# Low parts of 24 up-projection weight tiles by adding transfers, and weight sums on VectorE

## The chip, the cores and the metric

The kernel runs on one core of one Trainium2 chip. A core has five engines that work at the same time, each through its own list of instructions in order: TensorE (PE, matrix products; PEld is its loading of the stationary operand), VectorE (DVE), ScalarE (ACT), GpSimd (POOL) and SyncE (SP), which here only issues transfers. Transfers (DMA) move data between the device memory and the on-chip memory; a plain one is issued by SP here, one that adds to what already lies at its destination by GpSimd. Engines wait for each other through semaphores. The metric is the device time of one execution in microseconds (us); the median over several runs counts.

## The reference

One layer of a hybrid decoder: 512 tokens, 1024 channels, float32. A convolution branch and a gated linear attention branch run side by side and are merged, and a channel mixer follows. The change is in the mixer:

```python
u2 = _rmsnorm(h, norm2_g[l])
z = _causal_dwconv(u2 @ w_ffn_up[l], ffn_dw_w[l], ffn_dw_b[l])
h = h + (jax.nn.silu(z[..., :FFN_DIM]) * z[..., FFN_DIM:]) @ w_ffn_down[l]
```

FFN_DIM is 2816, so `w_ffn_up` is 1024 x 5632, that is 44 column tiles of 128. Tiles 0 to 21 give the half that goes through silu (called a here), tiles 22 to 43 the half that multiplies it (b); tile f and tile 22 + f belong together. The convolution in between has three taps over time.

## The kernel before

**Products in three parts.** TensorE multiplies in a rounded float32 format (fp32r). To keep precision, each operand is cut in a high part (the value rounded to fp32r) and a low part (what rounding left over). A product x y is then high x high + high x low + low x high, three matrix products in the same accumulator (`mm3`, lines 448 to 450). For an up tile of 1024 x 128 against 512 tokens, `col_tile` (line 452) makes 8 x 3 = 24 products of 128x512, in the order low weight, then twice high weight, for each of the eight blocks of 128 input channels.

**Weights.** Every weight tile is 128 x 1024 floats (512 KB). `load` (line 242) issues its transfer from SP into one of four `raw` buffers. `split_weight` (line 343) makes the two parts, `whi` and `wlo`, in four buffers each: ScalarE copies `raw` into `whi` with rounding (line 385, or 355 for tiles that belong to a pair or to the down projection), and VectorE subtracts `whi` from `raw` into `wlo` (line 390, or 356). For the tiles in the set `ADDED` (some tiles of the input projections) the low part is made otherwise: ScalarE writes the negated rounded value into `wlo` (line 387), and GpSimd issues a second transfer of the same weights that adds to it (line 388). So these tiles are loaded twice, and VectorE has no work for them.

```python
            if (name, spec) in ADDED:
                pace[0] = nc.scalar.mul(lo, raw, -1.0)
                nc.gpsimd.dma_start(lo, a[name][spec], accum_op=ALU.add)
            else:
                pace[0] = nc.vector.tensor_tensor(lo, raw, hi.bitcast(F32), ALU.subtract)
```

**Order.** `order` lists all weights in the order of use. `weight` (line 408) hands out the next one and calls `prefetch` so that two more (`LOOK`) behind it are split, in program order, ahead of the products that follow. `refill` then loads into free raw buffers.

**The up projection.** It is done in three groups (`GROUPS`, line 34) of four, three and four pairs of tile numbers; after each group comes the part of the down projection that uses it (`seven`, line 1370). `up_plan` (line 156) writes the order within a group by hand. The first members of the pairs, and a few more tiles, are plain: a and b each by `col_tile`. The second member q of most pairs is done together with its b tile by `two_tiles` (line 1171), which multiplies the two tiles by two halves of the tokens with seven products instead of eight, on sums and differences of the operands. Its four steps are called x1, x3, x2, x4; their products are 128x256. A unit interleaves these four steps with the pieces of two plain tiles. A unit that closes a group looks like this:

```python
                a1, a2, a3 = (("tile", a, ks) for ks in halves(3, 6))
                seq = [x1, a1, x3, a2, x2, a3, x4, ("second", q), ("tile", b, whole)]
```

so the b tile comes as a whole, directly after x4. In the order of weights it is x1, a, x3, x2, b, x4: b is split when x2 is handed out. In groups one and two these closing tiles are a = 8, b = 30 and a = 12, b = 34; in group three there is no closing unit, and plain tiles 19 and 41 end it. Groups two and three open with a plain tile a (9 and 13), followed by x1 of a pair.

**Weight sums of a pair.** The steps x3 and x4 need sums of quarters of the two raw weight tiles. `two_sums` (line 324) makes four sums of 128x512 per pair on GpSimd (line 327): three behind the split of x1, one behind the split of x3. Eight pairs of up tiles are done this way, and six pairs of merge weights earlier in the kernel.

**Behind the products.** ScalarE and VectorE read the accumulators: bias and three taps of the convolution (lines 1497 and 1500), silu (1508), product of the halves (1514), and then the high and low parts of the activations and of their sums for the down projection (`fsplit`, lines 1519 and 1520: the tiles yh and yl, ah and al, sh and sl, made from w, f and v; line 1530 makes the difference in w). ScalarE also copies partial results of a pair from the accumulators (line 1178), and VectorE combines them (1181). Accumulators are banks of PSUM: five of `mm` and three of `ax`.

Who comes first on an engine where program order does not say it is decided by a scheduling layer at build time; `tc.keep_in_program_order` and `tc.issue_after` tie single instructions to a place.

Of the kernel before, what the change touches and what calls it, by code (L numbers as in the profile page):

```python
# [10 lines left out]
F32 = mybir.dt.float32  # L11
# [6 lines left out]
P = 128  # L18
D = 1024
# [19 lines left out]
BEHIND = [_HALVES[:3], _HALVES[3:6], _HALVES[6:9], _HALVES[9:]]  # L39
BEHIND += [[("w_conv", m, half) for m in pair for half in range(2)] for pair in O_PAIRS[:2]]  # L40
MERGE_REST = [("w_conv", m) for pair in O_PAIRS[2:] for m in pair]
LOOK = 2

ADDED = {("w_glu", 2 * k) for k in range(2, KT)} | {("w_r", m) for m in range(KT)}
ADDED |= {("w_v", KT // 2 + j) for j in (0, 1)}
RATE = 5.0
WARM = (6, 3, 2)
MID = 4
# [27 lines left out]
def trunk_layer(ctx: ExitStack, tc: tile.TileContext, a: dict, out: bass.AP):  # L76
# [24 lines left out]
    def nm(s):  # L101
        return f"{s}_{next(names)}"
# [50 lines left out]
        nc.gpsimd.memset(att, 0.0)  # L153


    def up_plan(gi):


        pairs = GROUPS[gi]
        whole = range(KT)  # L160

        def halves(*cuts):
            return [range(a, b) for a, b in zip((0, *cuts), (*cuts, KT))]

        def unit(q, f, kind):

            a, b = f, FT + f
            x1, x3, x2, x4 = (("part", q, part) for part in ("x1", "x3", "x2", "x4"))
            a1, a2 = (("tile", a, ks) for ks in halves(4))
            if kind == "opens":  # L170
                b1, b2, b3 = (("tile", b, ks) for ks in halves(4, 6))
                seq = [a1, x1, a2, x3, b1, x2, b2, x4, ("second", q), b3]
            elif kind == "closes":
# [3 lines that stand above are left out]
                a1, a2 = (("tile", a, ks) for ks in halves(5))  # L177
                b1, b2 = (("tile", b, ks) for ks in halves(4))
                seq = [x1, a1, x3, a2, x2, b1, x4, ("second", q), b2]
            return seq + [("first", f)]  # L180

        firsts = [p for p, _ in pairs[1:]]
        if gi + 1 < len(GROUPS):
            firsts.append(GROUPS[gi + 1][0][0])
        plan = []
        n = 0
        if gi == 0:
            (p, q), (f, _) = pairs[1:3]
            for i, role in ((p, "first"), (q, "second"), (f, "first")):
                plan += [("tile", i, whole), ("tile", FT + i, whole), (role, i)]  # L190
            n = 2
        while n < len(firsts):
            last = n + 1 == len(firsts) and gi + 1 < len(GROUPS)
            kind = "closes" if last else "opens" if n == 0 else ""
            plan += unit(pairs[n][1], firsts[n], kind)
            n += 1
        if n < len(pairs):
            q = pairs[n][1]
            plan += [("tile", q, whole), ("tile", FT + q, whole), ("second", q)]
        return plan  # L200
# [123 lines left out]
    def two_sums(name, p, q, part):  # L324

        def add(out, x, y):
            work = nc.gpsimd.tensor_tensor(out, x, y, ALU.add)  # L327
            if name == "w_up":
                tc.keep_in_program_order(work)

        left, right = slice(0, T), slice(T, D)
        if part == "x1":
            one, two = pair_raws[name, p]
            three = raw_tile()
            pair_raws[name, p].append(three)
            add(three[:, left], one[:, left], two[:, left])
            add(three[:, right], three[:, left], two[:, right])
            add(two[:, left], two[:, left], two[:, right])
        if part == "x3":
            one, _, three = pair_raws[name, p]  # L340
            add(three[:, left], three[:, right], one[:, right])

    def split_weight(halves=False, between=None):

        if len(ready) < len(order):
            while len(raws) <= len(ready):
                load()
            raw = raws[len(ready)]
            name, spec = order[len(ready)]
            if name in SEVEN or name == "two":  # L350
                raw = operand(raw, *spec) if name in SEVEN else two_operand(*spec)
                n = raw.shape[-1]
                hi = wp.tile([P, D], F32R, tag="whi", name=nm("whi"), bufs=4)[:, :n]
                lo = wp.tile([P, D], F32R, tag="wlo", name=nm("wlo"), bufs=4)[:, :n]
                nc.scalar.copy(hi, raw)  # L355
                two_low[:] = [nc.vector.tensor_tensor(lo, raw, hi.bitcast(F32), ALU.subtract)]  # L356
                with ExitStack() as order_of:
                    for ins in behind:
                        order_of.enter_context(tc.issue_after(ins.ins))
                    sum_on(name, *spec) if name in SEVEN else two_sums(*spec)  # L360
                ready.append((hi, lo))
                refill()
                return
            hi = wp.tile([P, D], F32R, tag="whi", name=nm("whi"), bufs=4)
            if order[len(ready)][0] == "w_low":
                nc.scalar.copy(hi, raw)
                if order[len(ready)][1] == 0:
                    part_lo = lambda t: t.rearrange("p (k c) -> p k c", c=P)[:, :, :RANK]
                    nc.vector.tensor_tensor(part_lo(hi), part_lo(raw), part_lo(hi.bitcast(F32)), ALU.subtract)
                ready.append((hi, None))  # L370
                refill()
                return
            lo = wp.tile([P, D], F32R, tag="wlo", name=nm("wlo"), bufs=4)
            if halves:
                ready.append((hi, lo))

                def high(c):
                    nc.scalar.copy(hi[:, c], raw[:, c])

                def low(c):  # L380
                    nc.vector.tensor_tensor(lo[:, c], raw[:, c], hi[:, c].bitcast(F32), ALU.subtract)

                cols = [slice(j * T, (j + 1) * T) for j in range(2)]
                return [[lambda c=c, part=part: part(c) for c in cols] for part in (high, low)]
            nc.scalar.copy(hi, raw)  # L385
            if (name, spec) in ADDED:
                pace[0] = nc.scalar.mul(lo, raw, -1.0)  # L387
# [3 lines that stand above are left out]
            ready.append((hi, lo))  # L391
            refill()
# [6 lines left out]
    def third_ahead():  # L399

        n = used[0] + LOOK
        if n == len(ready) < len(order) and order[n][0] == "two" and order[n][1][-1] == "x3":
            split_weight()
            return two_low[0]

    two_low = []

# [44 lines left out]
    def col_tile(w, acts, acc=None, lo=0, hi=T, at={}, ks=range(KT)):  # L452

        if acc is None:
            acc = mm_bank()
        for k in ks:
            s = slice(k * P, (k + 1) * P)
            ah, al = acts[k]
            mm3(acc[:, lo:hi], (w[0][:, s], w[1][:, s]), (ah[:, lo:hi], al[:, lo:hi]), k == 0, k == KT - 1)
            if k in at:  # L460
                at[k]()
        return acc

    def row_half(name, j0, n, acts, nk, done, tok_inner, middle=None):

# [702 lines left out]

    combined = []

    def two_tiles(name, p, q, acts7, side_bank, at_once=False):

        x, y, z = mm_bank(), side_bank(), side_bank()
        c1, c2 = tmp(), tmp()
        t1, t2 = slice(0, H), slice(H, T)

# [13 lines left out]
        combine(c1[:, t1], c1[:, t1], z[:, :H], ALU.add)  # L1190
        yield
        w = weight("two", (name, p, q, "x3"))
        step(x, "n2", w, 1, False)
        put(c2[:, t1], x)
        step(y, "s1", w, 0, True)
# [429 lines left out]
    for gi, pairs in enumerate(GROUPS):  # L1625
# [26 lines left out]
        for what, i, *rest in up_plan(gi):  # L1652
            if what == "tile":
                if 0 in rest[0]:
                    banks[i] = (weight("w_up", i), mm_bank())
                wt, acc = banks[i]
                col_tile(wt, acts2, acc, ks=rest[0])
                if KT - 1 in rest[0] and i < FT:
                    values[i] = value(i, acc)
            if what == "part":  # L1660
                if rest[0] == "x1":
                    units[i] = two_tiles("w_up", i, FT + i, lambda: up_acts, ax_bank)
                done = next(units[i])
                if done:
                    values[i] = value(i, done[0])
                    banks[FT + i] = (None, done[1])
                    third = [taps_at[0], third_ahead()]
            if what == "first":
                w = first_gated(i, values.pop(i), banks.pop(FT + i)[1])
                if any(i in pair for pair in pairs):  # L1670
# [105 lines left out]
```

## Time and profile before

| | |
|---|---|
| median of 3 runs | 825.09 us (824.46 to 825.40) |
| profiled execution, its own time | 826.27 us |
| its span, first to last instruction | 824.5 us |
| TensorE busy | 816.3 us, 99% of the span |
| VectorE busy | 719.2 us, 87% |
| ScalarE busy | 449.8 us, 55% |
| GpSimd busy | 148.9 us, 18% |
| granted TensorE clock, mean of the span | 0.999 of full speed |
| data moved by DMA | 106.27 MB, 129 GB/s |

The page of the profile gives busy times of each engine, then the chain of work that ended last, followed back from the last instruction to what released each step, and then groups of instructions: line, engine, operation, output <- inputs with shapes, count, and behind the bar the busy time of the group in us, the mean time of one in ns, and the idle time of the engine just before them with who ended it. Rows of a timeline give start in us, duration in us, engine, line, operation and tiles; in brackets the idle time before and who ended it. Rows of windows give, for a stretch of time, its length and the busy time and count of each engine, the granted clock, the mean busy share of the DMA engines and GB/s. A matrix product's time in a row (0.39 us for 128x512) is longer than the step from one to the next (0.23 us), as they overlap.

### The profile page before, as it was taken

How to read it: one execution, taken by the hardware profiler on the slowest of the kernel's cores; microseconds unless marked ns; L12 is line 12 of the kernel's file. 1: busy time of each engine (PE TensorE's matmuls, PEld its weight loads, DVE VectorE, ACT ScalarE, POOL GpSimd, SP SyncE). 2: the span in 40 equal slices, each digit the busy share in tenths (PEclk: the TensorE clock that was granted, in tenths of full speed). 3: DMA queues.
4: the chain of work that ended last, by engine and by line, in shares of the span. 5: the costliest groups of instructions: out<-in, count | busy, mean ns of one | idle time of the engine just before them, and what ended most of it. 6: DMA issues, size and time to landing. Idle time of an engine off the chain costs nothing.

```text
span 824.5 us, 11562 instructions
## 1 busy us (share of the span) xinstructions
PE 816.3 (99%) x4323; PEld 705.8 (86%) x4323; DVE 719.2 (87%) x1165; ACT 449.8 (55%) x666; POOL 148.9 (18%) x133
## 2 busy tenths in 40 slices
PE   9999999999999999999999999999999999999996
PEld 8888888888888889999988898898889988899885
DVE  5689999998989699886788889989975999789896
ACT  6744446655654456684454546556435663456654
POOL 2000010001010213443001100230123301622012
PEclk9999999999999999999999999999999999999999
DMA  8355673553443103323647633055642457334662
GB/s 317 94 118 150 153 184 103 128 153 103 89 116 103 51 27 114 116 78 106 211 112 215 177 101 103 27 167 160 143 132 89 140 142 164 105 103 148 184 128 103
DMA packets 30616, 106.27 MB, mean 129 GB/s; under 512 B 3464, under 2 KB 3600, under 8 KB 30560
## 3 DMA queue, kind: packets, MB, share of 16 engines
q1 hardware_dynamic: 24784, 85.34, 30.3%
q0 software_dynamic: 5760, 20.19, 14.4%
q8 instruction: 34, 0.56, 0.3%
q14 instruction: 22, 0.18, 0.1%
q10 hardware_dynamic: 16, 0.00, 0.0%
HBM read 103.42 MB, written 2.10 MB: 128 GB/s over the span
## 4 chain that ended last, share of the span: by engine, by line
PE 98%; DMA 0%; ACT 0%; DVE 0%; POOL 0%; POOLq 0%; issue 0%; ACTq 0%
PE mm L448 28%; PE mm L449 28%; PE mm L450 28%; PE mm L662 3%; PE ax L450 2%; PE ax L449 2%; PE ax L448 2%; PE ax L1067 1%; PE ax L576 1%; PE ax L1048 1%; PE ax L1069 1%; PE ax L1035 1%; DMA x<-in_x_dram 0%; PE ax L529 0%; PE ax L1033 0%; PE ax L1082 0%
## 5 line engine op out<-in xcount | busy, mean ns | idle before, releaser
L448 PE MATMUL mm<-uh,wlo 128*128 128x512 f32 (+1 forms) x672 | 244.8, 364 | 0.0
L449 PE MATMUL mm<-ul,whi 128*128 128x512 f32 (+1 forms) x672 | 242.6, 361 | 0.0
L450 PE MATMUL mm<-uh,whi 128*128 128x512 f32 (+1 forms) x672 | 242.3, 361 | 0.0
L450 PEld LDWEIGHTS mm<-uh,whi 128*128 128x128 f32 x672 | 126.9, 189 | 19.4
L448 PEld LDWEIGHTS mm<-uh,wlo 128*128 128x128 f32 x672 | 127.0, 189 | 18.8
L449 PEld LDWEIGHTS mm<-ul,whi 128*128 128x128 f32 x672 | 127.1, 189 | 18.6
L385 ACT CAST whi<-raw 128x1024 fp32r<-128x1024 f32 x86 | 89.7, 1046 | 57.6 <-PE mm L450 29.7
L356 DVE TENSOR_TENSOR wlo<-raw,whi 128x1024 fp32r<-128x1024 f32 x80 | 95.0, 1195 | 24.4 <-ACT whi L355 20.5
L327 POOL TENSOR_TENSOR raw<-raw,raw 128x512 f32<-128x512 f32 x42 | 67.7, 1613 | 211.8 <-DVE wlo L356 116.4
L390 DVE TENSOR_TENSOR wlo<-raw,whi 128x1024 fp32r<-128x1024 f32 x70 | 91.7, 1313 | 14.6 <-ACT whi L385 14.6
L355 ACT CAST whi<-raw 128x1024 fp32r<-128x1024 f32 x80 | 76.3, 957 | 36.2 <-PE mm L450 27.3
L786 DVE SCALAR_TENSOR_TENSOR c<-h,pp,c 128x255 f32<-128x255 f32 (+14 forms) x120 | 57.1, 476 | 3.2 <-ACT c L782 3.0
L786 DVE SCALAR_TENSOR_TENSOR c<-aside,btmp,c 128x255 f32<-128x255 f32 (+14 forms) x120 | 57.1, 476 | 0.0
L786 DVE SCALAR_TENSOR_TENSOR aside<-h,pp,aside 128x255 f32<-128x255 f32 (+6 forms) x112 | 53.3, 476 | 0.0
L355 ACT CAST whi<-kept 128x1024 fp32r<-128x1024 f32 (+1 forms) x32 | 31.8, 996 | 33.6 <-DVE kept L310 16.8
L1500 DVE SCALAR_TENSOR_TENSOR tmp<-mm,pp,tmp 128x511 f32<-128x511 f32 (+1 forms) x56 | 41.4, 743 | 4.0 <-ACT tmp L1497 3.9
L356 DVE TENSOR_TENSOR wlo<-kept,whi 128x1024 fp32r<-128x1024 f32 (+1 forms) x32 | 37.0, 1155 | 5.2 <-ACT whi L355 5.0
L1178 ACT COPY tmp<-mm 128x256 f32<-128x256 f32 x48 | 17.6, 367 | 34.2 <-PE mm L450 33.6
L1416 DVE TENSOR_TENSOR hres<-hres,mm 128x512 f32<-128x512 f32 (+1 forms) x49 | 32.3, 672 | 4.0 <-PE mm L450 2.6
L1497 ACT ACTIVATE tmp<-mm,pp 128x512 f32<-128x512 f32 x28 | 21.8, 777 | 19.1 <-PE mm L450 18.9
L387 ACT ACTIVATE wlo<-raw 128x1024 fp32r<-128x1024 f32 x16 | 16.9, 1059 | 22.1 <-PE mm L448 22.1
L1500 DVE SCALAR_TENSOR_TENSOR tmp<-tmp,pp,tmp 128x511 f32<-128x511 f32 (+1 forms) x32 | 27.8, 887 | 0.4
(351 smaller groups left out, 1782.8 us busy)
## 6 DMA issues: line engine op xcount, KB each, us to landing
raw<-in_w_up_dram SPq DMA_DIRECT2D x44, 512.0 KB, 4.2
raw<-in_w_glu_dram SPq DMA_DIRECT2D x16, 512.0 KB, 4.5
raw<-in_w_down_dram SPq DMA_DIRECT2D x15, 512.0 KB, 4.3
kept<-in_w_down_dram POOLq DMA_DIRECT2D x10, 512.0 KB, 5.8
raw<-in_w_v_dram SPq DMA_DIRECT2D x8, 512.0 KB, 5.8
raw<-in_w_qk_dram SPq DMA_DIRECT2D x8, 512.0 KB, 3.3
raw<-in_w_r_dram SPq DMA_DIRECT2D x8, 512.0 KB, 4.6
wlo<-in_w_r_dram POOLq DMA_DIRECT2D x8, 512.0 KB, 8.2
```

What stands on the lines that cost most here:

```text
L327: work = nc.gpsimd.tensor_tensor(out, x, y, ALU.add)
L355: nc.scalar.copy(hi, raw)
L356: two_low[:] = [nc.vector.tensor_tensor(lo, raw, hi.bitcast(F32), ALU.subtract)]
L385: nc.scalar.copy(hi, raw)
L390: pace[0] = nc.vector.tensor_tensor(lo, raw, hi.bitcast(F32), ALU.subtract)
L448: nc.tensor.matmul(acc, ll, rh, start=first, stop=False, **kw)
L449: nc.tensor.matmul(acc, lh, rl, start=False, stop=False, **kw)
L450: nc.tensor.matmul(acc, lh, rh, start=False, stop=last, **kw)
L662: nc.tensor.matmul(acc, act, ready[k // 2][wi][:, j], start=first, stop=last)
L786: nc.vector.scalar_tensor_tensor(out[:, j:], x[:, : half_t - j], w, out[:, j:], ALU.mult, ALU.add)
L1416: done = nc.vector.tensor_tensor(hres[t, n][:, c], hres[t, n][:, c], acc[:, c], op)
L1500: nc.vector.scalar_tensor_tensor(z[:, s:], acc[:, : T - s], w[j], z[:, s:], ALU.mult, ALU.add)
```

## The change

1. 24 up tiles, a and b of f = 1, 3, 4, 5, 8, 9, 20, 12, 13, 16, 17, 19, join `ADDED`: all plain up tiles but the first four. For them ScalarE writes the negated rounded value into `wlo` first, GpSimd issues the transfer that adds the weights, and the cast into `whi` comes behind that.
2. The products of these tiles are made by a new function, `high_first`: for all eight channel blocks first the two products that use the high part of the weights, and at the end the eight that use the low part.
3. The four weight sums of each of the eight up pairs are made on VectorE and not on GpSimd, and are no longer tied to their place in program order. The merge pairs keep theirs on GpSimd.
4. The second side accumulator of a pair (`y`) is taken when x3 starts and not at x1.
5. A further way to treat pairs, in which all sums are made in place, comes with a function of its own (`split_in_place`), a plan for its units and a look-ahead for them (`next_ahead`), but is entered only for tiles in the set `BOTH`, which is empty. It is cut from the diff below.

```diff
+BOTH = ()
...
+ADDED |= {("w_up", m) for f in (1, 3, 4, 5, 8, 9, 20, 12, 13, 16, 17, 19) for m in (f, FT + f)}
...
+    with_both = set(BOTH)
...
     def two_sums(name, p, q, part):
 
         def add(out, x, y):
-            work = nc.gpsimd.tensor_tensor(out, x, y, ALU.add)
-            if name == "w_up":
-                tc.keep_in_program_order(work)
+            (nc.vector if name == "w_up" else nc.gpsimd).tensor_tensor(out, x, y, ALU.add)
...
+            if (name, spec) in ADDED and name == "w_up":
+                pace[0] = nc.scalar.mul(lo, raw, -1.0)
+                nc.gpsimd.dma_start(lo, a[name][spec], accum_op=ALU.add)
+                nc.scalar.copy(hi, raw)
+                ready.append((hi, lo))
+                refill()
+                return
             nc.scalar.copy(hi, raw)
             if (name, spec) in ADDED:
                 pace[0] = nc.scalar.mul(lo, raw, -1.0)
...
+    def high_first(w, acts, acc, which):
+
+        every = [(k, 0, p) for k in range(KT) for p in (1, 0)] + [(k, 1, 0) for k in range(KT)]
+        for n in which:
+            k, of_w, of_act = every[n]
+            w_k = w[of_w][:, k * P : (k + 1) * P]
+            nc.tensor.matmul(acc, w_k, acts[k][of_act], start=n == 0, stop=n == len(every) - 1)
...
-    def two_tiles(name, p, q, acts7, side_bank, at_once=False):
+    def two_tiles(name, p, q, acts7, side_bank, at_once=False, lazy=False):
 
-        x, y, z = mm_bank(), side_bank(), side_bank()
+        x, z = mm_bank(), side_bank()
+        y = None if lazy else side_bank()
...
         w = weight("two", (name, p, q, "x3"))
+        y = y or side_bank()
...
-                col_tile(wt, acts2, acc, ks=rest[0])
+                if ("w_up", i) in ADDED:
+                    high_first(wt, acts2, acc, range(3 * rest[0].start, 3 * rest[0].stop))
+                else:
+                    col_tile(wt, acts2, acc, ks=rest[0])
...
-                    units[i] = two_tiles("w_up", i, FT + i, lambda: up_acts, ax_bank)
+                    units[i] = two_tiles("w_up", i, FT + i, lambda: up_acts, ax_bank, lazy=True)
...
-                    third = [taps_at[0], third_ahead()]
+                    if i not in BOTH:
+                        third = [taps_at[0], next_ahead() if i in with_both else third_ahead()]
```

More of the change, by code (lines that the diff above doesn't have):

```diff
@@ L165, in unit @@
         def unit(q, f, kind):
+            if f in BOTH:
+                with_both.add(q)
+                turns = ((q, "x1"), (f, "x1"), (q, "x3"), (f, "x3"), (q, "x2"), (q, "x4"), (f, "x2"), (f, "x4"))
+                seq = [("part", i, part) for i, part in turns]
+                return seq[:6] + [("second", q)] + seq[6:] + [("first", f)]
             a, b = f, FT + f
@@ L341, in two_sums, with split_in_place, add, split @@
             add(three[:, left], three[:, right], one[:, right])
+    def split_in_place(hi, lo, name, p, q, part):
+        one, two = pair_raws[name, p]
+        left, right = slice(0, T), slice(T, D)
+        def add(x, y):
+            nc.vector.tensor_tensor(x, x, y, ALU.add)
+        def split(hi, lo, x):
+            nc.scalar.copy(hi, x)
+            two_low[:] = [nc.vector.tensor_tensor(lo, x, hi.bitcast(F32), ALU.subtract)]
+        if part == "x3":
+            split(hi[:, left], lo[:, left], one[:, left])
+            add(one[:, left], two[:, right])
+            add(two[:, left], two[:, right])
+            split(hi[:, right], lo[:, right], one[:, left])
+            add(one[:, right], one[:, left])
+            return
+        split(hi, lo, {"x1": one, "x2": two, "x4": one[:, right]}[part])
+        if part == "x1":
+            add(one[:, left], two[:, left])
     def split_weight(halves=False, between=None):
@@ L350, in split_weight @@
             if name in SEVEN or name == "two":
-                raw = operand(raw, *spec) if name in SEVEN else two_operand(*spec)
-                n = raw.shape[-1]
+                if name == "two" and spec[1] in with_both:
+                    n = T if spec[-1] == "x4" else D
+                else:
+                    raw = operand(raw, *spec) if name in SEVEN else two_operand(*spec)
+                    n = raw.shape[-1]
                 hi = wp.tile([P, D], F32R, tag="whi", name=nm("whi"), bufs=4)[:, :n]
                 lo = wp.tile([P, D], F32R, tag="wlo", name=nm("wlo"), bufs=4)[:, :n]
+                if name == "two" and spec[1] in with_both:
+                    split_in_place(hi, lo, *spec)
+                    ready.append((hi, lo))
+                    refill()
+                    return
                 nc.scalar.copy(hi, raw)
@@ L384, in split_weight @@
                 return [[lambda c=c, part=part: part(c) for c in cols] for part in (high, low)]
+            if (name, spec) in ADDED and name == "w_up":
+                pace[0] = nc.scalar.mul(lo, raw, -1.0)
+                nc.gpsimd.dma_start(lo, a[name][spec], accum_op=ALU.add)
+                nc.scalar.copy(hi, raw)
+                ready.append((hi, lo))
+                refill()
+                return
             nc.scalar.copy(hi, raw)
@@ L404, in third_ahead, with next_ahead @@
             return two_low[0]
+    def next_ahead():
+        n = used[0] + LOOK
+        if n == len(ready) < len(order):
+            two = order[n][0] == "two"
+            split_weight()
+            return two_low[0] if two else pace[0]
     two_low = []
@@ L1656, in trunk_layer @@
                 wt, acc = banks[i]
-                col_tile(wt, acts2, acc, ks=rest[0])
+                if ("w_up", i) in ADDED:
+                    high_first(wt, acts2, acc, range(3 * rest[0].start, 3 * rest[0].stop))
+                else:
+                    col_tile(wt, acts2, acc, ks=rest[0])
                 if KT - 1 in rest[0] and i < FT:
```

## The prediction, before the result was known

> **What bounds the kernel now.** I read the page first: engine totals, chain, groups. Then the same totals for the stretch that the change touches, 501 us (first plain tile of the list) to 815 us (end of the last down step).
>
> ```profile
> span 824.5 us, 11562 instructions
> ...
> PE 816.3 (99%) x4323; PEld 705.8 (86%) x4323; DVE 719.2 (87%) x1165; ACT 449.8 (55%) x666; POOL 148.9 (18%) x133
> ...
> PE 98%; DMA 0%; ACT 0%; DVE 0%; POOL 0%; POOLq 0%; issue 0%; ACTq 0%
> ...
> L385 ACT CAST whi<-raw 128x1024 fp32r<-128x1024 f32 x86 | 89.7, 1046 | 57.6 <-PE mm L450 29.7 <-issue 12.4 <-PE ax L450 7.5
> ...
> L327 POOL TENSOR_TENSOR raw<-raw,raw 128x512 f32<-128x512 f32 x42 | 67.7, 1613 | 211.8 <-DVE wlo L356 116.4 <-DVE wlo L390 41.0 <-DMA raw<-in_w_up_dram 34.8
> L390 DVE TENSOR_TENSOR wlo<-raw,whi 128x1024 fp32r<-128x1024 f32 x70 | 91.7, 1313 | 14.6 <-ACT whi L385 14.6
> ...
> L1416 DVE TENSOR_TENSOR hres<-hres,mm 128x512 f32<-128x512 f32 (+1 forms) x49 | 32.3, 672 | 4.0 <-PE mm L450 2.6 <-DMA hres<-in_x_dram 1.0
> ...
> L387 ACT ACTIVATE wlo<-raw 128x1024 fp32r<-128x1024 f32 x16 | 16.9, 1059 | 22.1 <-PE mm L448 22.1
> ```
>
> ```profile
> core 0: us, PE busy (x) PEld busy (x) DVE busy (x) ACT busy (x) POOL busy (x), PEclk, DMA share, GB/s
> 501.00:815.00 314.00, 314.00 (x1702) 273.13 (x1701) 278.40 (x366) 169.91 (x240) 71.69 (x54) 1.00 0.45 129
> ```
>
> The chain is 98% TensorE, and in the stretch TensorE is busy 314.00 of 314 us at a granted clock of 1.00. VectorE, though 278.40 us busy there, is never waited for long enough to leave a hole. So a lighter VectorE buys nothing by itself: the change can only keep this stretch closed or open holes in it.
>
> **The change, part by part.**
>
> *Plain low parts (24 tiles).* Removed: 24 VectorE subtractions, 24 x 1.313 = 31.5 us (row L390). Added: 24 negated copies on ScalarE, 24 x 1.059 = 25.4 us (row L387), and on GpSimd's queue 24 adding transfers of 512 KB. Nobody waits for the removed ones, so they give 0. ScalarE is idle 144 of the 314 us; the copies cost nothing while casts stay ahead. The tightest cast is that of tile 13, opening the third group:
>
> ```profile
> 701.00 1.06 ACT L385 CAST whi<-raw 128x1024 fp32r<-128x1024 f32 x1 [1.12 <-PE mm L450]
> 705.58 0.39 PE L448 MATMUL mm<-uh,wlo 128*128 128x512 f32 x1
> ```
>
> With the copy in front, the cast ends at 702.06 + 1.06 = 703.12, still 2.46 us before TensorE's 705.58. Behind it the next pair's cast also slides 1.06 us; its use is treated below.
>
> *Pair sums.* Eight up pairs of four sums: 32 sums leave GpSimd (32 x 1.613 = 51.6 us, or a little more) and go to VectorE. The trace has no such sum there; the nearest row, the same size with one operand in PSUM, is L1416 at 0.672 us: 32 x 0.672 = 21.5 us. Bounds: 0.41 us (a 256-wide sum, row 565.48 below) to 1.6 us (GpSimd's price); I take 0.67. VectorE's balance is 21.5 - 31.5 = -10.0 us. Moreover the subtractions beside GpSimd's sums were stretched:
>
> ```profile
> 545.77 2.67 POOL L327 TENSOR_TENSOR raw<-raw,raw 128x512 f32<-128x512 f32 x2 [6.41 <-DMA raw<-in_w_up_dram]
> 547.66 1.86 DVE L356 TENSOR_TENSOR wlo<-raw,whi 128x1024 fp32r<-128x1024 f32 x1
> 549.78 1.98 DVE L390 TENSOR_TENSOR wlo<-raw,whi 128x1024 fp32r<-128x1024 f32 x1
> ```
>
> They take 1.86 and 1.98 us there against 1.21 alone (row 565.82); that goes too. What is queued behind the new sums on VectorE: in the built order the three first sums stand ahead of the x1 subtraction of the pair that opens groups two and three. The third group is the tighter:
>
> ```profile
> 703.42 2.32 DVE L356 TENSOR_TENSOR wlo<-raw,whi 128x1024 fp32r<-128x1024 f32 x1
> 708.30 0.28 PE L448 MATMUL mm<-uh,wlo 128*128 128x256 f32 x1
> ```
>
> It ended at 705.74, 2.56 us early. Three sums add 2.0 us and a removed subtraction takes off 1.2, so its margin stays above 1.7 us. I book 0 for the sums; without this cover each would cost its 0.67 us.
>
> *High products first.* The same 24 products per tile, with the same weight loads; only the order changes. The eight that read the low part now come last, so the low part is due 16 products later. Steps are 0.23 us (573.75 to 573.97 below), so 3.6 us. Worth 0 on TensorE itself.
>
> *The second accumulator taken later* changes which of three banks is reused: 0, since that bank's reader finished a whole part earlier. The empty set leaves its branch unused: 0.
>
> *The landing* is the only unknown that can reach TensorE. A tile's chain is now copy 1.06, issue, landing, first low product. For transfers of this form, line L388 answers, from issue to landing:
>
> ```profile
> DMA to landing us min/median/max: 5.5/7.8/10.5
> ```
>
> For 21 of the 24 tiles the low product comes 10 us or more behind the end of the copy: nothing. (Tile 13: copy to 702.06; the low product near 712.1, which is 705.58 plus 16 products of 0.23 and an x1 part of 24 at 0.12 between them.) Three have less. Two are the b tiles that close groups one and two (column tiles 30 and 34, partners of 8 and 12): they are asked for only two parts ahead, and in the built order their copy stands behind the cast of the same tile and the casts sh and yh. For tile 30:
>
> ```profile
> 564.26 0.36 ACT L1178 COPY tmp<-ax 128x256 f32<-128x256 f32 x1
> 564.52 1.05 ACT L385 CAST whi<-raw 128x1024 fp32r<-128x1024 f32 x1
> 563.52 0.84 ACT L1519 CAST sh<-v 128x768 fp32r<-128x768 f32 x1 [1.74 <-DVE v L1542]
> 565.93 0.62 ACT L1519 CAST yh<-w 128x512 fp32r<-128x512 f32 x1 [0.35 <-DVE w L1530]
> ...
> 564.01 0.68 DVE L356 TENSOR_TENSOR wlo<-raw,whi 128x512 fp32r<-128x512 f32 x1
> 565.48 0.41 DVE L1530 TENSOR_TENSOR w<-w 128x256 f32<-128x256 f32 x1
> 565.82 1.21 DVE L390 TENSOR_TENSOR wlo<-raw,whi 128x1024 fp32r<-128x1024 f32 x1
> ...
> 570.32 0.40 PE L448 MATMUL mm<-uh,wlo 128*128 128x512 f32 x1
> ...
> 573.75 0.39 PE L448 MATMUL mm<-uh,wlo 128*128 128x512 f32 x1
> 573.97 0.39 PE L449 MATMUL mm<-ul,whi 128*128 128x512 f32 x1
> ```
>
> The copy of ax now stands ahead of sh and no longer waits behind it, so cast and sh are over by about 565.0. The difference w (565.48) now follows the x4 subtraction (564.01 + 0.68) directly and ends near 565.1; yh follows to 565.7, the copy to 566.6, issue at 566.65. The 17th product, first to read the low part, starts at 573.97: 7.3 us for the landing. At 7.8 it costs 0.5, at 10.5 3.2, at 5.5 nothing.
>
> ```profile
> 665.24 0.69 DVE L356 TENSOR_TENSOR wlo<-raw,whi 128x512 fp32r<-128x512 f32 x1
> ...
> 675.09 0.39 PE L449 MATMUL mm<-ul,whi 128*128 128x512 f32 x1
> ...
> 759.94 0.78 ACT L1497 ACTIVATE tmp<-mm,pp 128x512 f32<-128x512 f32 x1
> 760.62 1.03 ACT L385 CAST whi<-raw 128x1024 fp32r<-128x1024 f32 x1
> ...
> 772.25 0.39 PE L449 MATMUL mm<-ul,whi 128*128 128x512 f32 x1
> ```
>
> Tile 34 by the same steps: x4's subtraction ends at 665.93, w 0.4 and yh 0.6 and the copy 1.1 later, issue near 667.9, due at 675.09: 7.2 us. Loss 0.6 at 7.8, 3.3 at 10.5, none at 5.5. Tile 19, of the last plain pair: cast to 761.65, copy, issue near 762.7 at the latest, due at 772.25: 9.5 us; loss 0, 1.0 at 10.5.
>
> GpSimd's queue: the new transfers are issued in order with the adding transfers of the down weights, but those of tiles 30 and 34 come ahead of them and hold them up by one issue (under 1 us); none of the 24 stands behind a down transfer of its own group. SP's queue keeps its order; loads start earlier where a raw tile was held by a late subtraction.
>
> **Sum.** 0 (subtractions) + 0 (copies) + 0 (sums) + 0 (order) + 0.5 (tile 30) + 0.6 (tile 34) + 0 (tile 19) = +1.1 us, between 0 (landings of 5.5; below nothing it can't go, as TensorE has no hole to give back) and 3.2 + 3.3 + 1.0 = 7.5 (all at 10.5). The profiled execution took 826.27 us, 1.2 above the median of 825.09 of the runs shown; in it the sum gives 827.4, against the median 826.2. A measurement of this kernel can tell about 0.2%, 1.65 us, from no change; +1.1 is inside.
>
> [...]
>
> **Rivals.**
>
> 1. *Late landings decide (slower).* Place: first low product of tiles 30 and 34. When their copy ends, the freed raw tile starts a load too, and the two transfers run together:
>
> ```profile
> raw<-in_w_up_dram SPq DMA_DIRECT2D x44, 512.0 KB, 4.2
> ```
>
> If a load adds its whole 4.2 us to the shortest 5.5, the landing takes 9.7: 2.4 + 2.5 + 0.2 = 5.1 us, 830.2. It decides from a landing of 8.1 us on (0.8 + 0.9 = 1.7 us). For: the maximum of 10.5. Against: the median of 7.8, although such loads ran beside many of those 16 too. [...]
>
> 2. *The lighter VectorE pays (faster).* It would need holes that VectorE ends. The stretch has none visible in 314.00 us; what could be gained is a few tenths, 824.8. For a gain over 1.65 us the tail after the last product would have to shrink, and no instruction there changes.
>
> 3. *VectorE or ScalarE becomes late.* Sums at GpSimd's 1.6 us would add 3 x 1.6 - 1.2 = 3.6 us before tile 14's x1 subtraction, against 2.56 of margin: about 1 us in two groups at most, 827.1. Against it: all rows of plain sums of this width on VectorE are near 0.7.
>
> 4. *The change does nothing that counts.* All landings within 7.2 us: 825.1. This is the forecast's lower half.
>
> **How the numbers follow.** Loss of at most 1.65 us (forecast with rival 4): 0.57, with its own range 824.5 to 826.7. Rival 1 0.34, rival 3 0.05: slower 0.39. Rival 2 0.04. Time of the likeliest: 826.2. The range drops rival 2's half and the far end of rival 1: 824.6 to 829.6.
>
> **What would show it.** Right: TensorE still closed between 501 and 815 except for two holes under 1 us in front of low products, by the adding transfer, near 574 and 675; L327 on GpSimd down to the merge pairs; the sums on VectorE near 0.67 us; the subtractions near 1.2 everywhere; ScalarE up by some 25 us and VectorE down by 10 or more; landings of 6 to 8 us. Wrong: holes at other tiles, waits of TensorE for VectorE at a pair's x1, or landings above 8.1 us.

## The result, and the profile after

The changed kernel takes 829.37 us (median of 4, 828.87 to 829.44) against 824.78 us (median of 4, 824.38 to 825.4) for the kernel before: a ratio of 1.0054, 95% interval 1.0036 to 1.0071. (Here and below the ratio comes from all runs of a comparison, so it can differ in the last digits from the quotient of the two medians beside it.) It is slower by 4.6 us, more than the 1.65 us that a measurement can tell from no change. A later comparison of the same pair gave 829.33 (4 runs) and 825.4 us (19 runs), 1.0045, interval 1.003 to 1.006. The profiled execution after took 829.44 us, 1.74 us more than its span.

The page of the changed kernel: busy totals, the chain by engine, and the two kinds of transfer that carry up weights (KB each, median us from issue to landing).

```profile
span 827.7 us, 11621 instructions
...
PE 816.9 (99%) x4323; PEld 704.9 (85%) x4323; DVE 697.6 (84%) x1173; ACT 472.7 (57%) x690; POOL 114.0 (14%) x125
...
PE 94%; DMA 3%; ACT 1%; issue 1%; DVE 0%; POOL 0%; POOLq 0%; ACTq 0%
...
raw<-in_w_up_dram SPq DMA_DIRECT2D x44, 512.0 KB, 6.5
wlo<-in_w_up_dram POOLq DMA_DIRECT2D x24, 512.0 KB, 7.1
```

TensorE has the same 4323 products. Its share of the chain falls from 98% to 94%, and transfers take 3%: somewhere TensorE now waits for a transfer, or for work that stands behind one. Also new is the first of the two transfer rows: the ordinary loads of up weights, which the change doesn't touch, took 4.2 us in the median before and take 6.5 now.

The stretch from 501 to 815 us of the changed kernel, columns as in the prediction's row:

```profile
501.00:815.00 314.00, 311.38 (x1685) 269.72 (x1684) 255.66 (x370) 189.09 (x258) 37.27 (x44) 1.00 0.65 163
```

TensorE is busy 311.38 of 314 us instead of all of it. VectorE lost 22.7 us, ScalarE gained 19.2, GpSimd lost 34.4; the DMA engines are busy 0.65 of the time instead of 0.45. The waits of TensorE in the changed kernel say what ended the new holes (us in total, times, longest):

```profile
PE mm L502 <- ACT tmp L1241: 1.9, 2, 1.0
...
PE mm L524 <- DMA wlo<-in_w_up_dram: 0.7, 1, 0.7
```

One hole is of the kind that the prediction looked for, a low product that waits for its adding transfer. The other two are of a kind that it didn't price: ScalarE's copy out of an accumulator (L1241, the evacuation in `put`). Both kernels issue the same number of products, tile by tile in the same sequence (only the order within a tile differs), so the start of the k-th product can be compared. Apart from start-up, the difference jumps in three places only:

| place | shift ahead of it, us | behind it, us | step |
|---|---|---|---|
| start-up to tile 30's first low product | 0 | -0.46 | -0.46 |
| first low product of tile 30 (574.42 us after) | -0.46 | 0.59 | 1.05 |
| x3 part of unit 20 (643.05 us after) | 0.76 | 1.96 | 1.20 |
| x3 part of unit 16 (735.98 us after) | 2.01 | 3.19 | 1.18 |
| last product (820.80 after, 817.61 before) | 3.19 | 3.19 | 0 |

Smaller drifts in the down steps add 0.2. The three holes are 3.43 us together, and the two spans differ by 3.2.

How the hole at 643 comes about is read from the chain of the changed kernel (start, us, what):

```profile
633.41 6.72 DMA raw<-in_w_up_dram
...
640.22 0.07 ACT wlo L425
...
641.18 1.03 ACT whi L427
642.22 0.53 ACT tmp L1572
642.74 0.26 ACT tmp L1241
...
643.05 0.39 PE mm L502
```

The load of tile 42 takes 6.72 us. ScalarE's negated copy (L425) of this tile waits for it; the cast (L427) and a Silu (L1572) stand behind the copy, and behind them the evacuation (L1241) of the x1 part, whose accumulator TensorE needs for x3. The kernel before, at the same place (timeline of ScalarE, then of TensorE), and its load of the same tile (minimum, median and maximum of one transfer):

```profile
638.74 0.64 ACT L1508 ACTIVATE tmp<-tmp 128x512 f32<-128x512 f32 x1 [0.70 <-DVE tmp L1500]
639.27 0.35 ACT L1178 COPY tmp<-mm 128x256 f32<-128x256 f32 x1
639.53 1.05 ACT L385 CAST whi<-raw 128x1024 fp32r<-128x1024 f32 x1
```

```profile
641.18 0.28 PE L448 MATMUL mm<-xq,wlo 128*128 128x256 f32 x1
```

```profile
DMA to landing us min/median/max: 3.2/3.2/3.2
```

There the evacuation was over 1.6 us before TensorE needed it, the cast of tile 42 stood behind it, and the load took 3.2 us. Two things changed: the order on ScalarE, and the time of the load, which was issued at the same moment (633.2 and 633.4 us) but now 0.56 us behind the adding transfer of tile 20 (issued 632.85, landed 6.8 us later, at 639.6; the load landed at 640.1). Side by side both transfers are slow (6.7 us where the load took 3.2 before, 6.8 us where the quickest of the 24 adding transfers took 5.4), and they end within 0.5 us of each other. Tile 38 in unit 16 is the same picture: a load of 6.68 us, then copy, cast, Silu and evacuation in the same order.

### The profile page after: what moved, and what is told of

Its sections match the earlier page's. It is cut to its first block, busy times and chain, and to the rows that moved or that the text cites. A ratio compares the mean times of both kernels' runs of the same rounds, so it can differ in the third digit from the quotient of the medians.

```text
span 827.7 us, 11621 instructions
## 1 busy us (share of the span) xinstructions
PE 816.9 (99%) x4323; PEld 704.9 (85%) x4323; DVE 697.6 (84%) x1173; ACT 472.7 (57%) x690; POOL 114.0 (14%) x125
## 4 chain that ended last, share of the span: by engine, by line
PE 94%; DMA 3%; ACT 1%; issue 1%; DVE 0%; POOL 0%; POOLq 0%; ACTq 0%
PE mm L502 22%; PE mm L503 22%; PE mm L504 22%; PE mm L524 14%; PE mm L724 3%; PE ax L502 2%; PE ax L503 2%; PE ax L504 2%; DMA raw<-in_w_up_dram 2%; DMA wlo<-in_w_up_dram 1%; PE ax L1129 1%; PE ax L638 1%; PE ax L1131 1%; PE ax L1110 1%; PE ax L1097 1%
## 5 line engine op out<-in xcount | busy, mean ns | idle before, releaser
L502 PE MATMUL mm<-uh,wlo 128*128 128x512 f32 (+1 forms) x480 | 169.4, 353 | 0.0
L504 PE MATMUL mm<-uh,whi 128*128 128x512 f32 (+1 forms) x480 | 167.4, 349 | 0.0
L503 PE MATMUL mm<-ul,whi 128*128 128x512 f32 (+1 forms) x480 | 167.2, 348 | 0.0
L395 DVE TENSOR_TENSOR wlo<-raw,whi 128x1024 fp32r<-128x1024 f32 x80 | 92.0, 1155 | 36.2 <-ACT whi L394 32.8
L504 PEld LDWEIGHTS mm<-uh,whi 128*128 128x128 f32 x480 | 90.7, 189 | 11.8
L394 ACT CAST whi<-raw 128x1024 fp32r<-128x1024 f32 x80 | 76.1, 959 | 38.0 <-PE mm L504 30.1
L431 ACT CAST whi<-raw 128x1024 fp32r<-128x1024 f32 x62 | 64.6, 1046 | 43.8 <-PE mm L504 30.4
L524 PE MATMUL mm<-uh,whi 128*128 128x512 f32 x192 | 75.1, 391 | 0.0
L524 PE MATMUL mm<-ul,whi 128*128 128x512 f32 x192 | 74.9, 390 | 0.0
L436 DVE TENSOR_TENSOR wlo<-raw,whi 128x1024 fp32r<-128x1024 f32 x46 | 57.2, 1248 | 11.4 <-ACT whi L431 11.4
L426 POOL DMA_DIRECT2D wlo<-in_w_up_dram x24 | 20.7, 863 | 214.0 <-ACT wlo L425 166.4
L524 PE MATMUL mm<-uh,wlo 128*128 128x512 f32 x192 | 48.4, 391 | 0.7 <-DMA wlo<-in_w_up_dram 0.7
```

Source lines behind the costliest of these rows:

```text
L502: nc.tensor.matmul(acc, ll, rh, start=first, stop=False, **kw)
L503: nc.tensor.matmul(acc, lh, rl, start=False, stop=False, **kw)
L504: nc.tensor.matmul(acc, lh, rh, start=False, stop=last, **kw)
L524: nc.tensor.matmul(acc, w_k, acts[k][of_act], start=n == 0, stop=n == len(every) - 1)
```

## The experiments

Theory A: one hole is tile 30's late landing; the other two need both the slowed load and the copy and cast ahead of the evacuation. Rivals: the sums on VectorE are the cause (V); the order alone costs it (O); a late load is paid somewhere anyway (L). All diffs are against the changed kernel. The first four runs stand beside runs of the kernel before only; where their expectations speak of 829.4 us, that is the result above.

**The two halves of the change, alone.**

```
-ADDED |= {("w_up", m) for f in (1, 3, ..., 19) for m in (f, FT + f)}
```

> Only the pair sums are on VectorE; the 24 plain tiles keep their subtractions. Theory A (the changed kernel's loss is made by the adding transfers: a landing that is too late before tile 30's low part, and two copies of ScalarE that wait for slowed loads of tiles 42 and 38): no hole over 0.3 us between 501 and 815 us, time within 0.6 us of the kernel before (about 824.8). Rival V (VectorE's new sums delay what TensorE waits for at the x3 parts of units 20 and 16): two holes of about 1.1 us stay there, about 827.

Measured: 825.26 us (10 runs) against 825.51 (31 runs), ratio 1.0001, interval 0.999 to 1.0012. Waits of TensorE, the loads, and the stretch of 501 to 815 us:

```profile
PE mm L501 <- DVE hres L1479: 0.9, 1, 0.9
```

```profile
raw<-in_w_up_dram SPq DMA_DIRECT2D x44, 512.0 KB, 3.5
```

```profile
501.00:815.00 314.00, 313.07 (x1696) 272.00 (x1695) 281.25 (x397) 168.95 (x238) 18.35 (x22) 1.00 0.45 129
```

Theory A expected no hole over 0.3 us; there is one of 1.1 us, at 701 us in the down step. The chain ahead of it begins with the late landing of a down weight, followed by its cast, its low part and VectorE's addition (`hres`), for which TensorE waits:

```profile
690.88 9.28 DMA kept<-in_w_down_dram
```

It comes and goes between executions: it is as large in two of the later traces (the slower of two landings there took 9.3, 9.1 and 9.4 us in these three), and only 0.1 us in the changed kernel's first one (8.3 us). The two holes at x3 are not there: V falls, and moving the sums alone is no change. The loads land in 3.5 us, so it isn't the sums that slow them.

```
-            (nc.vector if name == "w_up" else nc.gpsimd).tensor_tensor(out, x, y, ALU.add)
+            work = nc.gpsimd.tensor_tensor(out, x, y, ALU.add)
+            if name == "w_up":
+                tc.keep_in_program_order(work)
```

> Only the adding transfers (with their product order); the pair sums stay on GpSimd, whose queue also issues the transfers. Theory A: the three holes of the changed kernel stay, and transfers that are queued behind a pair's sums go out up to 3 us later, so 829 to 832. Rival V: without the sums on VectorE the two holes at x3 go: 827 or less.

Measured: 826.52 us (10 runs), ratio 1.0015, interval 1.0005 to 1.0025. Theory A's expectation missed and V's number came: tile 30's hole is 0.5 us, and those at x3 fell to 0.26 and 0.08 us with the sums back on GpSimd. Taken by itself this speaks for V, which the run above refutes. ScalarE's timeline shows what happened instead:

```profile
639.62 1.07 ACT L427 ACTIVATE wlo<-raw 128x1024 fp32r<-128x1024 f32 x1 [2.35 <-DMA raw<-in_w_up_dram]
640.59 0.62 ACT L1574 ACTIVATE tmp<-tmp 128x512 f32<-128x512 f32 x1
641.11 0.35 ACT L1243 COPY tmp<-mm 128x256 f32<-128x256 f32 x1
641.36 1.05 ACT L429 CAST whi<-raw 128x1024 fp32r<-128x1024 f32 x1
```

The wait for the load is there as before (2.35 us), but the scheduling layer put the cast (L429) behind the evacuation: the queue ahead of it is 1.03 us shorter, and about that much of the hole went. So for these two holes the sums matter by the order that the scheduling layer makes around them. Tile 30's transfer took 8.35 us to land here (8.1 in the changed kernel), so VectorE's sums aren't what makes it late. The theory missed a further loss of some 1.3 us in the down step of group two, where TensorE waits 0.5 us for a low part from VectorE (L397).

**The load alone.** The order is kept, the company is taken away.

```
+                c = slice(0, 16 if spec in (20, 16) else D)
-                nc.gpsimd.dma_start(lo, a[name][spec], accum_op=ALU.add)
+                nc.gpsimd.dma_start(lo[:, c], a[name][spec][:, c], accum_op=ALU.add)
```

> The changed kernel with the same instructions in the same order, but the adding transfers of tiles 20 and 16 move only 16 of their 1024 columns (the low parts of these two tiles are not those of the reference). Theory A, its first half (the load of the next tile is slow because the adding transfer runs beside it): the loads of tiles 42 and 38 land in about 3.2 us instead of 6.7, ScalarE's copies no longer wait for them, and the two holes at x3 fall from 1.1 to under 0.2 us each; 2.2 us less, about 827.1. Rival O (the place of the copy and the cast ahead of the evacuation costs the time by itself, whatever the load does): the two holes stay near 1.1 us, about 829.4.

Measured: 826.76 us (10 runs), ratio 1.0022, interval 1.001 to 1.0033; TensorE waits only for tile 30's transfer. The load of tile 42 and ScalarE's timeline:

```profile
DMA to landing us min/median/max: 3.4/3.4/3.4
```

```profile
637.97 1.06 ACT L425 ACTIVATE wlo<-raw 128x1024 fp32r<-128x1024 f32 x1 [0.61 <-PE ax L503]
638.93 1.04 ACT L428 CAST whi<-raw 128x1024 fp32r<-128x1024 f32 x1
639.88 0.62 ACT L1573 ACTIVATE tmp<-tmp 128x512 f32<-128x512 f32 x1
640.41 0.35 ACT L1242 COPY tmp<-mm 128x256 f32<-128x256 f32 x1
```

Copy and cast stand ahead of the evacuation as in the changed kernel, and both holes at x3 are gone: with the load at 3.4 us the evacuation ends in time. O falls. The time is near what theory A said (827.1).

**The order alone.** The load keeps its company, the queue is changed.

```
+                with tc.issue_after(puts[0].ins) if spec in (42, 38) else ExitStack():
                     pace[0] = nc.scalar.mul(lo, raw, -1.0)
                     nc.gpsimd.dma_start(lo, a[name][spec], accum_op=ALU.add)
                     nc.scalar.copy(hi, raw)
...
-            nc.scalar.copy(c, acc[:, :H])
+            puts[:] = [nc.scalar.copy(c, acc[:, :H])]
```

> The changed kernel with only this moved on ScalarE: the negated copy and the cast of tiles 42 and 38 stand behind the evacuation that the x3 part waits for. Theory A, its second half (the wait reaches TensorE only because the evacuation is queued behind the waiting copy): the loads still take about 6.7 us, but both holes at x3 go, 2.2 us less, about 827.1; only the hole before tile 30's low part stays. Rival L (the late load or the later copy is paid anyway, at tile 42's and 38's own products): the holes move there, about 829.4.

Measured: 826.43 us (10 runs), ratio 1.0011, interval 1.0001 to 1.0021. The load, and ScalarE's timeline:

```profile
DMA to landing us min/median/max: 7.0/7.0/7.0
```

```profile
639.53 0.63 ACT L1574 ACTIVATE tmp<-tmp 128x512 f32<-128x512 f32 x1 [1.71 <-DVE tmp L1566]
640.07 0.35 ACT L1243 COPY tmp<-mm 128x256 f32<-128x256 f32 x1
640.50 1.06 ACT L426 ACTIVATE wlo<-raw 128x1024 fp32r<-128x1024 f32 x1
641.47 1.03 ACT L428 CAST whi<-raw 128x1024 fp32r<-128x1024 f32 x1
```

The time is 0.7 us below what theory A said. The load is as slow as in the changed kernel, 7.0 us, and the copy no longer stands in anyone's way; the holes are gone and turn up nowhere else. L falls. Undoing either half is enough to remove these two holes, so they need both.

**The same kernel again, and the repairs together.**

> The changed kernel once more, beside the following ones on one chip. Theory A: again one hole of about 1.0 us before tile 30's first low product and two of about 1.1 us at the x3 parts of units 20 and 16, 3.4 us in all, so 3 to 4.6 us above the kernel before. Rival R (the holes are an accident of one execution): one or more of the three is missing, and the time is within 2 us of the kernel before.

Measured: 829.33 us (4 runs), ratio 1.0045, interval 1.003 to 1.006. All three holes are there again (1.0, 1.3 and 1.1 us), so R falls; a fourth, of 0.9 us, stands in the down step, as in the run with the sums alone. The waits put it down to ScalarE's copy (`wlo`), but VectorE's addition (`hres`) ended 0.15 us ahead of the product here too, as in that run.

```profile
PE mm L502 <- ACT tmp L1241: 1.8, 2, 1.0
...
PE mm L502 <- ACT wlo L425: 0.8, 1, 0.8
PE mm L524 <- DMA wlo<-in_w_up_dram: 0.7, 1, 0.7
```

The order of the run above, and tile 30 plain:

```
+ADDED -= {("w_up", 30)}
```

> Copy and cast of tiles 42 and 38 behind the evacuation, as in the earlier run, and tile 30 plain again (a subtraction on VectorE instead of the adding transfer). Theory A: all three holes are gone and nothing is gained otherwise, since TensorE was closed before: within 0.8 us of the kernel before. Rival B (the lighter VectorE pays once the holes are gone): 1 us or more below it. Rival L2 (other adding transfers are late behind them): 1.5 us or more above it.

Measured: 825.7 us (10 runs) against 825.4, ratio 0.9998, interval 0.9989 to 1.0008. The three holes are gone; the one in the down step (1.2 us) is in this trace. Both B and L2 fall.

The order of the run above, all 24 tiles by adding transfers, and tile 30's copy ahead of its cast:

```
-                    nc.scalar.copy(hi, raw)
+                    with tc.issue_after(pace[0].ins) if spec == 30 else ExitStack():
+                        nc.scalar.copy(hi, raw)
```

> All 24 tiles by adding transfers; copy and cast of tiles 42 and 38 behind the evacuation, and for tile 30 the negated copy ahead of its own cast and ahead of yh. Theory A: tile 30's transfer is issued about 1.3 us earlier (near 564.9 instead of 566.3 us), lands in about 8 us again, and its hole falls from 1.0 to under 0.2 us: within 0.8 us of the kernel before. Rival P (the landing is set by what runs beside it, not by the issue: it ends near 574 us whenever it begins): the hole stays near 1 us, and the time 1 us above.

Measured: 825.15 us (10 runs) against 825.4, ratio 0.9997, interval 0.9988 to 1.0006. The stretch, tile 30's copy on ScalarE, and its transfer, issued at 564.29 us:

```profile
501.00:815.00 314.00, 314.00 (x1706) 273.34 (x1706) 257.87 (x376) 190.50 (x262) 37.18 (x44) 1.00 0.65 164
```

```profile
562.83 1.06 ACT L426 ACTIVATE wlo<-raw 128x1024 fp32r<-128x1024 f32 x1
```

```profile
DMA to landing us min/median/max: 7.5/7.5/7.5
```

Issued 2.0 us earlier than in the changed kernel (1.3 expected) it landed at 571.8, ahead of its use: P falls. The stretch is closed again, and the whole change then gains nothing: with TensorE at 314.00 of 314 us there is nothing to gain. The second accumulator taken later is in this kernel too, so it costs nothing either.

**The product order.**

```
-                if ("w_up", i) in ADDED:
+                if False:
                     high_first(wt, acts2, acc, range(3 * rest[0].start, 3 * rest[0].stop))
```

> The changed kernel without the new product order: the products that read the low part stand at their old places among the others. Theory A: the low part of each plain tile is due 3.6 us earlier; tile 30's hole grows from 1.0 to about 4.6 us and tile 34, which had 1.6 us of room, opens one of about 2 us: profiled span 833 us or more. Rival H (the order doesn't matter, since transfers land early enough): no new hole, 828 us.

Measured: 852.77 us in one run, span 851.1. Theory A's direction is right and its size, 833, far too small. Waits of TensorE, and stretches in and behind its first long hole, behind a shorter one that ended at 686 us, and in and behind the second long one (columns as above; the third number from the end is TensorE's granted clock):

```profile
PE mm L502 <- DMA wlo<-in_w_up_dram: 19.9, 10, 4.4
```

```profile
569.60:572.20 2.60, 0.00 (x0) 0.00 (x0) 2.56 (x4) 2.60 (x6) 0.87 (x2) 1.00 1.03 180
572.30:579.00 6.70, 5.06 (x12) 4.01 (x13) 4.00 (x6) 1.31 (x2) 0.65 (x1) 0.50 0.98 217
579.10:584.00 4.90, 4.90 (x23) 4.01 (x23) 1.07 (x2) 1.89 (x3) 0.86 (x1) 1.00 0.20 25
686.00:691.00 5.00, 5.00 (x22) 4.15 (x23) 4.28 (x7) 1.64 (x3) 0.00 (x0) 1.00 0.98 233
720.30:722.40 2.10, 0.00 (x0) 0.00 (x0) 2.10 (x4) 0.35 (x1) 0.00 (x0) 1.00 1.05 275
722.50:729.20 6.70, 5.44 (x13) 4.28 (x14) 1.04 (x2) 2.00 (x2) 0.86 (x1) 0.50 0.36 102
```

Ten tiles now wait for their transfer, 19.9 us in all. The first, tile 30's of 4.4 us, is near what was expected (4.6), and so is tile 34's of 2.2 (2). The expectation missed eight others because most tiles are worked on in two or three pieces with parts of a pair between: to have the low products last puts them off by the parts as well, not by 3.6 us alone. A granted clock of 0.50 in and behind the two longest holes adds some 4.8 us, an estimate from the rows above; the rest of the loss comes from each wait setting the products back by a few tenths more than the idle time that the profile counts (1.05 for 0.75 us at tile 30 in the changed kernel).

## Why the prediction was right or wrong

The time, 829.4 us, lies in the range (824.6 to 829.6), but the likeliest case, a loss within 0.2%, is not what came; the case "slower" with 0.39 is. That the time fell in the range is luck: the sum had +1.1 us, the range reached so far up only for rival 1's late landings, and two of the three holes came by a path that the prediction booked at 0. By its own signs it was partly wrong: there are holes at other tiles (the x3 parts of units 20 and 16), none near 675 us, and landings above 8.1 us (up to 11.1, in the row below).

*The bound.* Right: TensorE was closed, and only holes could change the time. The repaired kernel has the full relief on VectorE and GpSimd and ends within 0.1% of before.

*VectorE and GpSimd.* Right. Three groups of the changed kernel in the stretch:

```profile
L395 DVE TENSOR_TENSOR wlo<-raw,whi 128x1024 fp32r<-128x1024 f32 x39 | 47.3, 1220 | 18.6 <-ACT whi L394 16.6 <-ACT tmp L1572 1.4 <-issue 0.6
...
L425 ACT ACTIVATE wlo<-raw 128x1024 fp32r<-128x1024 f32 x22 | 23.3, 1058 | 16.3 <-PE ax L502 9.4 <-DMA raw<-in_w_up_dram 6.7 <-PE mm L503 0.2
...
L337 DVE TENSOR_TENSOR raw<-raw,raw 128x512 f32<-128x512 f32 x24 | 16.5, 687 | 4.8 <-DMA raw<-in_w_up_dram 4.5
```

A sum takes 0.687 us (0.672 taken), a subtraction 1.22 (1.21), a copy 1.058 (1.059). VectorE's balance was put at -10 us "moreover" the stretching; it was -22.7. ScalarE's busy time rose by 22.9 us over the span for the 25.4 booked: its rows overlap by 0.1 us where one follows directly on another (640.22 + 1.06 against 641.18). In this trace nobody waited for any of it, as said.

*The copies on ScalarE: the step that failed.* "ScalarE is idle 144 of the 314 us; the copies cost nothing while casts stay ahead." Only casts were looked at, and only the tightest. The row L425 above has the missing item: ScalarE stood idle 6.7 us in front of copies that waited for loads. What is queued behind a waiting copy on its engine, the evacuation that TensorE needs at x3, was not named. Two units paid 1.20 + 1.18 = 2.4 us; the sum had 0 for it.

*The queues: the same step's other half.* "SP's queue keeps its order; loads start earlier where a raw tile was held by a late subtraction." The order held, but the sentence priced only when loads start, not how long they take beside 12.6 MB more of transfers (24 of 512 KB): 6.5 us instead of 4.2. Rival 1 even had the pair running together, and asked only what the load does to the adding transfer, never the reverse.

*The landings.* That a landing could hold up a low product was right, its sizes half so. Tile 30: issue at 566.26 us (566.65 estimated), room 7.25 us (7.3), landing 8.1: 1.05 us for a term of 0.5. Tile 34: issue at 669.81 us, which less the shift of 1.96 is 667.85 (667.9 estimated); landing 5.6, hole none, for a term of 0.6. Tile 19: landed 1.9 us ahead of its use; 0, as said. Together 1.05 for 1.1: the landing term was right, by two errors that cancel.

```profile
DMA to landing us min/median/max: 5.4/7.1/11.1
```

That row is for all 24 in the changed kernel; 5.5/7.8/10.5 was taken from the kernel before.

*High products first* was booked at 0, which holds for TensorE's work but hides that this part carries the change: without it the kernel took 852.8 us in its one run. "3.6 us" was mis-sized for all tiles that are cut in pieces.

*The rivals.* Rival 1's 830.2 us is nearest in time, but of its 5.1 us only 1.05 came, from one tile. Rival 3 named ScalarE, with another place (a pair's x1) and VectorE's sums as its cause; neither is so. Rivals 2 and 4 fall.

*What stays open.* The holes explain 3.4 of the 4.6 us between the medians (3.9 in the second comparison). The profiled execution of the kernel before took 826.27 us, 1.5 above the median that it stands against here, and start-up (up to 1.5 us) and the hole in the down step (up to 1.2 us) differ between executions; where the rest lies in the unprofiled ones wasn't seen.

## What to carry to other kernels

Before moving work to an engine with idle time, write down for every moved instruction what it waits for and what stands behind it in that engine's queue; idle time is of no use to an evacuation that is queued behind a wait (1.20 and 1.18 us lost here). Price new transfers twice: for their own landing, and for what they do to the loads that start beside them (6.7 us instead of 3.2 here), and read the second as a new due time for everything that waits for those loads. When the bounding engine is closed, taking work off the others can at best be no change (825.15 us against 825.4 here, with all holes closed).

## What the runs showed of the hardware that wasn't expected

- A load of 512 KB that starts 0.56 us behind an adding transfer of the same size lands in 6.7 to 7.0 us instead of 3.2; with an adding transfer of 8 KB in its place it lands in 3.4. The small adding transfer itself took 3.7 us, against 5.4 for the quickest of 512 KB: only 1.7 us of the 5.4 came with the 64 times larger size.
- With the sums on VectorE and all subtractions kept, VectorE's busy time in the stretch rose by 2.9 us only (278.40 to 281.25), though 32 sums at 0.69 us are 22 us: by this difference, an estimate, some 19 us of its time before was stretching that went away with GpSimd's sums (subtractions of 128x1024 took 1.31 and 1.41 us in the mean before, and take 1.22 in the changed kernel).
- TensorE's clock, in the run with the low products at their old places (rows above): in idle times of 4.4 and 3.6 us the granted clock fell to 0.50, 2.7 and 2.2 us after the last product, and stayed there for 6.8 us each time, 5.1 and 5.5 of them with products: 12 in 5.06 us and 13 in 5.44, so one in 0.42 us, where the step is 0.23 at a clock of 1.00. That cost some 2.4 us each time (an estimate: 12 or 13 products at 0.19 us more), besides the hole. Behind an idle time of 2.2 us the clock stayed at 1.00 (row from 686 us). What sets the moments of the fall and of the return, these two holes do not show.
